# Normalization, gate chain and convolution sums rewritten in the front of a two-layer hybrid block

## Chip, cores and metric

The kernel runs on one core of a Trainium2 chip. The metric is the device time of one execution in microseconds (us); where several executions were timed, their median counts.

## The reference, cut to what matters

512 tokens (256 context, 256 latent) of width 1024 go through two layers. In the second layer the context is only read, so everything after the keys and values is computed for the 256 latent tokens alone. Each layer is

```python
h = rmsnorm(x, norm1_g) * (1.0 + sc1) + sh1
a, mq, mk, mv, mo, mg, dq, dk, dv = jnp.split(h @ w_in, splits, axis=-1)
conv_l = conv_module(a, conv_w, conv_b, conv_ln_g, conv_ln_b)
mlstm_l = mlstm_mixer(...)            # gates: ig + bias, log_sigmoid(fg + bias), scans over time
diff_l = diff_mixer(...)
x = x + g1 * (jnp.concatenate([conv_l, mlstm_l, diff_l], axis=-1) @ w_out)
h2 = rmsnorm(x, norm2_g) * (1.0 + sc2) + sh2
x = x + g2 * peer_ffn(h2, peer_wq, peer_keys, peer_u, peer_v)
```

The convolution module is a depthwise convolution of 31 taps over time on 256 channels, followed by a layer norm and SiLU:

```python
u = a[..., :CONV_W] * jax.nn.sigmoid(a[..., CONV_W:])
y = lax.conv_general_dilated(u, conv_w, ...) + conv_b      # 31 taps, one filter per channel
return jax.nn.silu(layernorm(y, ln_g, ln_b))
```

The modulation vectors sc1, sh1, g1, ... are products of a conditioning vector with six 1024 x 1024 blocks of a matrix ("ada").

## The kernel before

Activations lie with channels on the 128 partitions and tokens along the free axis: `x[:, c, t]` is chunk c (of 8) of 128 channels, and a "half" is 256 tokens, so one operation of the norm has the shape 128x256. Every product runs in split precision: an operand v is kept as hi = v rounded to fp32r and lo = v - hi, and TensorE makes three matmuls of 128x512 or 128x256 (hi x hi, lo x hi, hi x lo) for each chunk. `wsplit` (L210) makes the two parts of a weight block: ScalarE writes whi (L218), GpSimd subtracts to give wlo (L219), one pair for each 128x512 half block. A Tile scheduler orders the instructions of each engine when the program is built, and each engine then works through its own list in that order.

Each layer has a front (`front`, L346) and an expert stage (`peer`). The front does, in order:

- `norm_mod` (L276 to L286): for each of 8 chunks and each half, four operations on four engines' turns: VectorE multiplies x by the reciprocal root (L282), ScalarE applies scale and shift (L283), GpSimd copies the result, rounded, to hh (L284), VectorE subtracts to give hl (L285). It is called twice per layer: n1 ahead of the input projection, n2 ahead of the expert stage (two halves for n1 of both layers and n2 of layer 0, one half for n2 of layer 1).
- `projg`: the four first blocks of the projection (gates, two blocks of convolution gates, one of convolution values) together, into banks "f", "f", "f", "d" of PSUM; matmuls L311 to L313.
- `gate_rows` (L488 to L553): the gates' block (128x512 in PSUM, of which 64 rows are input gates and 64 forget gates) becomes log-sigmoid sums. VectorE adds the bias (L497) and moves the forget rows down (L498), ScalarE takes Abs, Exp, Ln, Exp (L500 to L506), VectorE forms the log sigmoid (L502 to L509), splits it and the input gate into hi and lo by adding and subtracting a constant (L513 to L515), runs scans (L524, L528) and subtracts (L532, L533). TensorE then transposes the two results (L548); a second path makes `rows` (L542), which the mLSTM reads through the matmul at L590. Its scratch T1 shares the buffer of "v", T2 that of "vx".
- Further projections (`proj`, L297 to L299), among them the output gates and, in layer 0 only, `late()` (L1159), which computes three blocks of the modulation with `ada_rows` (L181) through the PSUM bank "a".
- `conv` (L460 to L485): for each of two blocks b of 128 channels one tensor_scalar (L465) and 30 scalar_tensor_tensor (L468) on VectorE, each adding one shifted and weighted copy of `up` to the sum cy in SBUF (128x512 in layer 0, 128x256 in layer 1); then TensorE sums over channels (L472), and the layer norm follows.
- `mlstm`: per head rows,sel (L590), the exponentials E (L598 ScalarE, L602 VectorE, L604, GpSimd's mask L606), the products mq,km (L611), VectorE's E times product (L616), the sums E,vx (L622). Then `diff`, `w_out` with the residual (L443) and sums of squares, and `norm_mod` again.

The order of these steps is the string 'kmcvkk0k123' (k keys, m mLSTM, c convolution, v values, digits the heads of differential attention), and the scheduler interleaves them. PSUM in the front has eight banks: f three, d two, m two, a one. The lines that the change touches are L282 to L285, L460 to L475, L488 to L517 and L1161.

## Time and profile before

| | us |
|---|---|
| median of 3 runs | 2994.78 (2994.21 to 3012.2) |
| the profiled execution, its own time | 3002.47 |
| span of the profiled execution, first to last instruction | 3000.3 |
| TensorE busy in the span | 2884.3 (96%) |
| mean granted TensorE clock | 0.981 |

The fronts of the two layers lie at about 0 to 430 us and 1915 to 2215 us of the span, the expert stages behind each. In the rows, PE is TensorE's matmuls, PEld its weight loads, DVE VectorE, ACT ScalarE, POOL GpSimd. "hh, whi" are operands by the program's names; f, d, m and a are the four kinds of PSUM bank. A matmul's duration overlaps with its neighbours', so the distance of two starts is what one costs.

### The profile page before, as it was taken

What the parts mean: (1) busy time and instruction counts of PE and PEld (TensorE: products, weight loads), DVE (VectorE), ACT (ScalarE), POOL (GpSimd) and SP (SyncE); (2) the same over time, 40 slices, a digit from 0 to 9 for tenths busy, and PEclk for the clock granted to TensorE, in tenths of its full rate; (3) what the DMA queues carried; (4) which work ended last, traced back from release to release, by engine and by line L of the source; (5) the groups of instructions that cost most, each with busy time, mean ns of one, the idle gap of its engine ahead of it and who ended that gap; (6) DMA issues with size and microseconds to landing.
All of it is one profiled execution on the core that took longest, in us unless ns stands there. A gap on an engine that the chain in (4) does not pass through costs nothing.

```text
span 3000.3 us, 43088 instructions
## 1 busy us (share of the span) xinstructions
PE 2884.3 (96%) x14960; PEld 2409.7 (80%) x14960; DVE 2009.4 (67%) x4447; ACT 1422.2 (47%) x2862; POOL 1075.4 (36%) x887
## 2 busy tenths in 40 slices
PE   7899999999999999999999999989989999999998
PEld 4575578888888888888888888777789999888887
DVE  4956537875666665566666665586659888666665
ACT  4344443336566665332333323345455666555554
POOL 4333255566666666000000000253478877000000
PEclk9899899999999999999999999999999999999999
DMA  6511134444555555867677776121255877998873
GB/s 234 189 64 36 35 113 137 127 137 164 211 183 204 189 188 213 283 238 249 235 242 239 242 247 216 34 83 52 78 178 175 277 255 272 309 314 270 267 233 125
DMA packets 257866, 565.60 MB, mean 189 GB/s; under 512 B 18336, under 2 KB 119200, under 8 KB 254448
## 3 DMA queue, kind: packets, MB, share of 16 engines
q1 hardware_dynamic: 256928, 560.42, 55.3%
q8 instruction: 118, 1.93, 0.3%
q0 software_dynamic: 720, 2.43, 0.2%
q14 instruction: 100, 0.82, 0.1%
HBM read 464.21 MB, written 98.57 MB: 188 GB/s over the span
## 4 chain that ended last, share of the span: by engine, by line
PE 76%; DVE 7%; DMA 1%; POOL 1%; ACT 1%; issue 1%; SPq 0%; DVEq 0%; ACTq 0%; POOLq 0%
PE h L864 10%; PE h L865 10%; PE h L866 10%; PE acc L1138 8%; PE acc L1139 8%; PE acc L1140 8%; PE acc L969 4%; PE acc L970 4%; PE acc L971 4%; PE f L813 3%; DVE cy L468 1%; PE f L311 1%; PE f L312 1%; PE f L313 1%; DMA v<-in_peer_v 1%
## 5 line engine op out<-in xcount | busy, mean ns | idle before, releaser
L847 POOL TENSOR_TENSOR ul<-u,uh 128x512 fp32r<-128x512 f32 x464 | 610.5, 1325 | 335.0 <-ACT uh L846 317.1
L864 PE MATMUL h<-hh,uh 128*128 128x512 f32 (+1 forms) x2048 | 692.4, 338 | 2.6 <-ACT ga L870 2.5
L866 PE MATMUL h<-hh,ul 128*128 128x512 f32 (+1 forms) x2048 | 689.6, 337 | 5.2 <-POOL ul L847 5.2
L865 PE MATMUL h<-hl,uh 128*128 128x512 f32 (+1 forms) x2048 | 689.9, 337 | 0.0
L846 ACT ACTIVATE uh<-u 128x512 fp32r<-128x512 f32 x512 | 319.3, 629 | 468.6 <-PE h L865 345.7
L866 PEld LDWEIGHTS h<-hh,ul 128*128 128x128 f32 x2048 | 389.5, 190 | 46.6 <-POOL ul L847 5.7
L864 PEld LDWEIGHTS h<-hh,uh 128*128 128x128 f32 x2048 | 389.9, 190 | 43.6 <-ACT ga L870 4.2
L865 PEld LDWEIGHTS h<-hl,uh 128*128 128x128 f32 x2048 | 389.9, 190 | 37.0
L1138 PE MATMUL acc<-vh,wh 128*128 128x512 f32 x1024 | 398.6, 389 | 1.1 <-ACT ga L870 1.1
L1139 PE MATMUL acc<-vl,wh 128*128 128x512 f32 x1024 | 398.6, 389 | 0.0
L1140 PE MATMUL acc<-vh,wl 128*128 128x512 f32 x1024 | 398.5, 389 | 0.0
L815 DVE TENSOR_REDUCE rt_stg<-f 128x256 f32<-128x512 f32 x384 | 244.9, 686 | 225.2 <-PE f L813 224.4
L219 POOL TENSOR_TENSOR wlo<-wt,whi 128x512 fp32r<-128x512 f32 x164 | 231.1, 1420 | 247.2 <-ACT whi L218 231.0
L1103 ACT ACTIVATE wh<-gb 128x512 fp32r<-128x512 f32 x128 | 80.7, 632 | 463.3 <-PE acc L1139 451.4
L375 POOL MEMSET up<- 128x60 f32 (+1 forms) x2 | 0.3, 148 | 718.0 <-PE acc L991 718.0
L1104 DVE TENSOR_TENSOR wl<-gb,wh 128x512 fp32r<-128x512 f32 x128 | 88.8, 695 | 236.9 <-ACT wh L1103 236.8
L1138 PEld LDWEIGHTS acc<-vh,wh 128*128 128x128 f32 x1024 | 192.2, 188 | 41.4 <-ACT ga L870 1.5
L1140 PEld LDWEIGHTS acc<-vh,wl 128*128 128x128 f32 x1024 | 192.2, 188 | 39.8
L1139 PEld LDWEIGHTS acc<-vl,wh 128*128 128x128 f32 x1024 | 192.2, 188 | 39.7
L846 ACT ACTIVATE vh<-v 128x512 fp32r<-128x512 f32 x256 | 155.7, 626 | 140.8 <-PE acc L971 81.4
L801 DVE SCALAR_TENSOR_TENSOR rt_oh_g<-iotap,rt_sT,rt_sg 128x256 fp32r<-128x256 f32 x512 | 213.3, 474 | 0.1
L969 PE MATMUL acc<-vh,wh 128*128 128x512 f32 x512 | 198.9, 390 | 1.3 <-ACT vh L846 1.3
(322 smaller groups left out, 5417.8 us busy)
## 6 DMA issues: line engine op xcount, KB each, us to landing
u<-in_peer_u SPq DMA_DIRECT2D x256, 512.0 KB, 4.0
v<-in_peer_v SPq DMA_DIRECT2D x256, 512.0 KB, 5.0
G<-rt_stg SPq DMA_DIRECT2D x24, 2048.0 KB, 6.9
act<-ga SPq DMA_DIRECT2D x180, 256.0 KB, 2.9
gb<-act SPq DMA_DIRECT2D x180, 256.0 KB, 3.7
g<-G SPq DMA_DIRECT2D x32, 1024.0 KB, 5.5
wa<-in_ada_t SPq DMA_DIRECT2D x56, 512.0 KB, 4.4
w<-in_ada_w SPq DMA_DIRECT2D x20, 1024.0 KB, 6.0
```

The source lines that it names most:

```text
L219: nc.gpsimd.tensor_sub(lo, raw, hi)
L801: nc.vector.scalar_tensor_tensor(og[:, k], self.iotap[:, None, :].to_broadcast([128, 2, 128]), sT[:, 1, c:c + 1], sg[:, c, :, None].bitcas ...
L815: nc.vector.tensor_reduce(stg[:, :, t4 + k2:t4 + k2 + 2].rearrange("p j t -> p t j"), pg.rearrange("p (t x j) -> p t j x", t=2, x=2), axis ...
L846: nc.scalar.activation(hi, raw[:, k * 512:(k + 1) * 512], AF.Copy)
L847: lo_eng.tensor_sub(lo, raw[:, k * 512:(k + 1) * 512], hi)
L864: nc.tensor.matmul(o, uh, hh[:, c, c0:], start=c == 0, stop=False)
L865: nc.tensor.matmul(o, uh, hl[:, c, c0:], start=False, stop=False)
L866: nc.tensor.matmul(o, ul, hh[:, c, c0:], start=False, stop=c == NB - 1)
L969: nc.tensor.matmul(A, wh[:, t], vh, start=s0, stop=False)
L1138: nc.tensor.matmul(A, wh[:, t], vh, start=s0, stop=False)
L1139: nc.tensor.matmul(A, wh[:, t], vl, start=False, stop=False)
L1140: nc.tensor.matmul(A, wl[:, t], vh, start=False, stop=s1)
```

## The change

The norm is made in three operations: VectorE forms x times A times the reciprocal root (one scalar_tensor_tensor), ScalarE adds the shift B and writes hh rounded, VectorE forms (u + B) - hh. GpSimd has no part in it.

The convolution adds up its taps in PSUM bank "a" instead of cy. In layer 0 each block b needs a whole bank, so the second block's sums begin when ScalarE has copied the first block's to cy; in layer 1 both blocks share one bank. ScalarE copies each sum to cy (Copy, two per layer).

The gate chain reads the PSUM block directly: ScalarE's Abs with the bias, VectorE twice at 64 rows (input gate + bias; forget gate + bias, minimum with 0). The input gate is split ahead of the log sigmoid; three later operations are merged into others. The scratch lies in two tiles of the buffer "PT" instead of that of "vx".

The late modulation of layer 0 uses the PSUM banks "d" instead of "a".

```diff
--- before.py
+++ after.py
@@ -279,10 +279,9 @@
         for c in range(NB):
             for o, t, s in self.halves(c0):
                 u = self.w(T, "nm", fam="r")
-                nc.vector.tensor_mul(u, self.x[:, c, t], rs[o])
-                nc.scalar.activation(u, u, AF.Identity, bias=B[:, c, s:s + 1], scale=A[:, s, c:c + 1])
-                nc.gpsimd.tensor_scalar(hh[:, c, t], u, 1.0, 0.0, op0=OP.mult, op1=OP.add)
-                nc.vector.tensor_sub(hl[:, c, t], u, hh[:, c, t])
+                nc.vector.scalar_tensor_tensor(u, self.x[:, c, t], A[:, s, c:c + 1], rs[o], op0=OP.mult, op1=OP.mult)
+                nc.scalar.activation(hh[:, c, t], u, AF.Identity, bias=B[:, c, s:s + 1])
+                nc.vector.scalar_tensor_tensor(hl[:, c, t], u, B[:, c, s:s + 1], hh[:, c, t], op0=OP.add, op1=OP.subtract)
         return hh, hl
 
 
@@ -461,12 +460,16 @@
         nc = self.nc
         ys = [self.frontp.tile([128, n], F32, name=f"cy{b}") for b in range(2)]
         for b in range(2):
-            y = ys[b].rearrange("p (s t) -> p s t", t=T)
+            if n * b % 512 == 0:
+                bank = self.ps("a")
+            sums = bank[:, n * b % 512:n * b % 512 + n]
+            y = sums.rearrange("p (s t) -> p s t", t=T)
             nc.vector.tensor_scalar(y, up[:, b, :, 0:T], P["conv_w"][:, b, 0:1], P["conv_b"][:, b:b + 1],
                               op0=OP.mult, op1=OP.add)
             for k in range(1, CONV_K):
                 nc.vector.scalar_tensor_tensor(y, up[:, b, :, k:k + T], P["conv_w"][:, b, k:k + 1], y,
                                          op0=OP.mult, op1=OP.add)
+            nc.scalar.activation(ys[b], sums, AF.Copy)
         mu = self.ps("a")[:, :n]
         for b in range(2):
             nc.tensor.matmul(mu, self.ones, ys[b], start=b == 0, stop=b == 1)
@@ -490,31 +493,31 @@
 
         nc, F = self.nc, self.frontp
         T1 = F.tile([128, 4, TT], F32, name="gr1", tag="v")
-        T2 = F.tile([64, 4, TT], F32, name="gr2", tag="vx")
-        G = T1[:, 0]
+        T2, T3 = (F.tile([64, 2, TT], F32, name=k, tag="PT", bufs=2) for k in ("gr2", "gr3"))
         Fg, e, u = (T1[0:64, k] for k in (1, 2, 3))
-        r, L, Bl, M = (T2[:, k] for k in range(4))
-        nc.vector.tensor_scalar(G, ps, P["gate_b"][:, 0:1], None, op0=OP.add)
-        nc.vector.tensor_copy(Fg, G[64:128])
-        ig = G[0:64]
-        nc.scalar.activation(e, Fg, AF.Abs)
+        r, L, Bl, M = T2[:, 0], T2[:, 1], T3[:, 0], T3[:, 1]
+        b = P["gate_b"]
+        nc.scalar.activation(e, ps[64:128], AF.Abs, bias=b[64:128, 0:1])
         nc.scalar.activation(e, e, AF.Exp, scale=-1.0)
-        nc.vector.tensor_scalar(u, e, 1.0, None, op0=OP.add)
-        nc.scalar.activation(L, u, AF.Ln)
-        nc.vector.tensor_scalar(r, u, -1.0, None, op0=OP.add)
-        nc.vector.tensor_sub(r, e, r)
-        nc.scalar.activation(u, L, AF.Exp, scale=-1.0)
-        nc.vector.tensor_mul(r, r, u)
-        nc.vector.tensor_add(L, L, r)
-        nc.vector.scalar_tensor_tensor(L, Fg, 0.0, L, op0=OP.min, op1=OP.subtract)
-        lh, ll, ih, il = e, u, r, Fg
+        ig = T1[0:64, 0]
+        nc.vector.tensor_scalar(ig, ps[0:64], b[0:64, 0:1], None, op0=OP.add)
+        nc.vector.tensor_scalar(Fg, ps[64:128], b[64:128, 0:1], 0.0, op0=OP.add, op1=OP.min)
 
         def split(hi, lo, v):
             nc.vector.tensor_scalar(hi, v, SPLIT, None, op0=OP.add)
             nc.vector.tensor_scalar(hi, hi, SPLIT, None, op0=OP.subtract)
             nc.vector.tensor_sub(lo, v, hi)
+        ih, il = r, ig
+        split(ih, il, ig)
+        nc.vector.tensor_scalar(u, e, 1.0, None, op0=OP.add)
+        nc.scalar.activation(L, u, AF.Ln)
+        nc.vector.scalar_tensor_tensor(e, u, -1.0, e, op0=OP.add, op1=OP.subtract)
+        nc.scalar.activation(u, L, AF.Exp, scale=-1.0)
+        nc.vector.tensor_mul(e, e, u)
+        nc.vector.tensor_sub(L, L, e)
+        nc.vector.tensor_sub(L, Fg, L)
+        lh, ll = e, u
         split(lh, ll, L)
-        split(ih, il, ig)
 
         def scan(dst, src, op):
             for d in range(2):
@@ -1158,7 +1161,7 @@
 
                 def late():
                     for w in (2, 4, 3):
-                        self.ada_rows(0, P[0], w, ("kT", "qT"), "a", "a")
+                        self.ada_rows(0, P[0], w, ("kT", "qT"), "d", "d")
                 h = self.front(l, P[l], c0, late if l == 0 else None)
 
             def side():
```

In the rows below and in the prediction the line numbers are those of the kernel before; in lists of the changed kernel they are one lower between the norm and the convolution's head (L296 for L297) and three higher behind it (L593 for L590). gr is the gates' scratch, ident the identity for the transposes, up the padded convolution input, a the PSUM bank.

VectorE, layer 1, from the gates' first operation to the middle of the chain. Before:

```order
L497 TENSOR_SCALAR gr_17497<-f,small_127 128x512
L498 COPY gr_17497<-gr_17497 64x512
L382 TENSOR_TENSOR up<-d,sg 128x256
L465 TENSOR_SCALAR cy_18305<-up,small_127 128x256
L468 SCALAR_TENSOR_TENSOR cy_18305<-up,small_127,cy_18305 128x256 x4
L502 TENSOR_SCALAR gr_17497<-gr_17497 64x512
L382 TENSOR_TENSOR up<-f,sg 128x256
L504 TENSOR_SCALAR gr_17498<-gr_17497 64x512
L468 SCALAR_TENSOR_TENSOR cy_18305<-up,small_127,cy_18305 128x256
L505 TENSOR_TENSOR gr_17498<-gr_17497,gr_17498 64x512
```

The same place of the changed kernel:

```order
L503 TENSOR_SCALAR gr_17453<-f,small_127 64x512
L504 TENSOR_SCALAR gr_17453<-f,small_127 64x512
L507 TENSOR_SCALAR gr_17454<-gr_17453 64x512
L512 TENSOR_SCALAR gr_17453<-gr_17453 64x512
L508 TENSOR_SCALAR gr_17454<-gr_17454 64x512
L514 SCALAR_TENSOR_TENSOR gr_17453<-gr_17453 64x512
L509 TENSOR_TENSOR gr_17453<-gr_17453,gr_17454 64x512
L381 TENSOR_TENSOR up<-d,sg 128x256
L467 TENSOR_SCALAR a<-up,small_127 128x256
L381 TENSOR_TENSOR up<-f,sg 128x256
```

The split of the input gate (L507 to L509) now stands at the front of the chain, ahead of the first tap, and only 8 taps instead of 11 stand between the chain's first operation and the subtraction that the transposes wait for (L532, now L535).

TensorE, layer 1, about the start of the mLSTM (rows,sel). Before:

```order
L590 MATMUL m<-rows,sel 128x256 x2
L472 MATMUL a<-cy_18305,ones 128x256
L472 MATMUL a<-cy_18306,ones 128x256
L339 MATMUL f<-rp_t,perm 128x256
L297 MATMUL f<-hh,whi 128x256
```

The changed kernel, the same place, and the rows to which the convolution's sums over channels went:

```order
L593 MATMUL m<-rows,sel 128x256 x2
L338 MATMUL f<-rp_t,perm 128x256
L296 MATMUL f<-hh,whi 128x256
...
L625 MATMUL m<-E,vx 128x256
L593 MATMUL m<-rows,sel 128x256
L328 MATMUL f<-wlo,hh 128x256
L475 MATMUL a<-cy_18261,ones 128x256
L475 MATMUL a<-cy_18262,ones 128x256
```

The two matmuls that read cy moved 51 rows back, behind the first head's sums E,vx.

TensorE, layer 1, about the first transposes of the gates. Before:

```order
L297 MATMUL f<-hh,whi 128x512
L298 MATMUL f<-hl,whi 128x512
L548 MATMUL m<-ident,gr_17498 128x64 x4
L299 MATMUL f<-hh,wlo 128x512
L297 MATMUL f<-hh,whi 128x512
```

After the change, the row of the transposes and its neighbours:

```order
L297 MATMUL f<-hl,whi 128x512
L298 MATMUL f<-hh,wlo 128x512
L551 MATMUL m<-ident,gr_17454 128x64 x4
L296 MATMUL f<-hh,whi 128x512
L297 MATMUL f<-hl,whi 128x512
```

The transposes stand 8 projection matmuls earlier in layer 1 (behind 18 of the 128x512 matmuls that lie behind the 128x256 ones instead of 26) and 9 earlier in layer 0.

VectorE, layer 1, the taps behind `rows` in the changed kernel; before, 43 taps of both blocks stood here in turn, and then the layer norm's first operation (L474) ahead of the first E (L602):

```order
L545 TENSOR_TENSOR rows<-gr_17453,rows 64x1024
L470 SCALAR_TENSOR_TENSOR a<-up,small_127,a 128x256 x17
L467 TENSOR_SCALAR a<-up,small_127 128x256
L470 SCALAR_TENSOR_TENSOR a<-up,small_127,a 128x256 x24
L340 TENSOR_TENSOR rp_u<-f,rope 128x256
L605 TENSOR_SCALAR E<-m,ah 128x128
```

The last six taps of the second block stand behind the first E, between operations of the mLSTM.

## Rows read from the trace of the kernel before

**Rows 1.** Page, busy time, share of the span and instructions of each engine.

```profile
PE 2884.3 (96%) x14960; PEld 2409.7 (80%) x14960; DVE 2009.4 (67%) x4447; ACT 1422.2 (47%) x2862; POOL 1075.4 (36%) x887
```

**Rows 2.** Windows: stretch, its length, busy us of each engine, PEclk, DMA share, GB/s.

```profile
0.00:430.00 430.00, 375.41 (x1639) 257.17 (x1640) 262.11 (x480) 191.78 (x414) 164.32 (x184) 0.93 0.33 115
430.00:1900.00 1470.00, 1467.67 (x6772) 1221.99 (x6771) 956.67 (x2257) 633.79 (x1297) 479.27 (x337) 1.00 0.60 203
1900.00:2230.00 330.00, 287.38 (x1692) 242.40 (x1692) 217.35 (x453) 162.88 (x339) 163.68 (x159) 0.94 0.26 81
...
150.00:175.00 25.00, 24.93 (x121) 18.88 (x121) 6.69 (x15) 9.82 (x24) 12.13 (x11) 1.00 0.27 85
...
2020.00:2040.00 20.00, 13.21 (x63) 10.23 (x63) 15.61 (x27) 8.35 (x22) 11.57 (x13) 0.83 0.36 105
```

**Rows 3.** Waits of PE, 0 to 430: us in total, times, longest.

```profile
PE m L548 <- DVE gr L532: 8.8, 1, 8.8
PE f L311 <- POOL hh L284: 8.7, 2, 6.0
```

**Rows 4.** Waits of PE, 1900 to 2230, the same columns.

```profile
PE m L548 <- DVE gr L532: 11.3, 1, 11.3
PE f L311 <- POOL hh L284: 9.4, 2, 5.2
PE a L472 <- DVE cy L468: 6.8, 1, 6.8
PE f L311 <- ACT rt_q L690: 3.1, 2, 2.9
```

**Rows 5.** Timeline 1935.8 to 1945: start, us, engine, instruction, idle before and releaser.

```profile
1935.91 1.97 DVE L282 TENSOR_TENSOR nm<-x,rsx 128x256 f32<-128x256 f32 x5
1936.38 2.57 ACT L283 ACTIVATE nm<-nm,mod,A 128x256 f32<-128x256 f32 x5 [2.64 <-DVE nm L282]
1937.06 2.69 POOL L284 TENSOR_SCALAR hh<-nm 128x256 fp32r<-128x256 f32 x5 [1.98 <-ACT nm L283]
...
1938.20 0.80 PE L311 MATMUL f<-hh,whi 128*128 128x512 f32 x1 [5.21 <-POOL hh L284]
...
1941.30 0.63 PE L311 MATMUL f<-hh,whi 128*128 128x512 f32 x1
1941.73 0.63 PE L312 MATMUL f<-hl,whi 128*128 128x512 f32 x1
...
1944.60 0.39 PE L311 MATMUL f<-hh,whi 128*128 128x512 f32 x1
1944.82 0.39 PE L312 MATMUL f<-hl,whi 128*128 128x512 f32 x1
```

**Rows 6.** Timeline of DVE, 1960 to 2031, the same columns.

```profile
1961.14 0.75 DVE L497 TENSOR_SCALAR gr<-f,small 128x512 f32<-128x512 f32 x1 [7.93 <-PE f L313]
...
1964.16 2.05 DVE L468 SCALAR_TENSOR_TENSOR cy<-up,small,cy 128x256 f32<-128x256 f32 x4
...
1978.30 2.88 DVE L514 TENSOR_SCALAR gr<-gr 64x512 f32<-64x512 f32 x2
1981.10 2.35 DVE L515 TENSOR_TENSOR gr<-gr,gr 64x512 f32<-64x512 f32 x2
...
1988.30 0.68 DVE L532 TENSOR_TENSOR gr<-gr 64x512 f32<-64x512 f32 x1
...
2001.78 27.95 DVE L468 SCALAR_TENSOR_TENSOR cy<-up,small,cy 128x256 f32<-128x256 f32 x43
```

**Rows 7.** Timeline of POOL, 1955 to 2032, the same columns.

```profile
2013.99 8.59 POOL L219 TENSOR_TENSOR wlo<-wt,whi 128x512 fp32r<-128x512 f32 x3 [5.58 <-ACT whi L218]
```

**Rows 8.** Lines, 1900 to 2230: xcount, busy us, mean ns, idle before.

```profile
L468 DVE SCALAR_TENSOR_TENSOR cy<-up,small,cy 128x256 f32<-128x256 f32 x60 | 39.5, 702 | 0.6
L616 DVE SCALAR_TENSOR_TENSOR E<-m,ea,E 128x256 f32<-128x256 f32 x24 | 10.6, 478 | 5.2 <-PE m L611 4.6 <-POOL E L606 0.7
...
L237 DVE TENSOR_SCALAR m<-m 128x256 f32<-128x256 f32 x7 | 3.0, 430 | 8.3 <-ACT y L236 8.3
```

## The prediction

> **What bounds the kernel now.** I read the page's busy times first, then the windows, then TensorE's waits stretch by stretch, then timelines of the places that the waits name. TensorE is busy 96% of the span [rows 1]. The windows show where the missing 4% is: between 430 and 1900 us it is busy 1467.67 of 1470.00 us at a granted clock of 1.00 and nothing that other engines do can be worth anything there; in the two fronts it is busy 375.41 of 430.00 and 287.38 of 330.00 at clocks of 0.93 and 0.94 [rows 2]. So the change, all of which lies in the fronts (and in the norm ahead of each expert stage), can only win from some 97 us of idle time (54.6 and 42.6) and from the lower clock.
>
> TensorE's waits in the fronts say which of that the change can reach: 8.8 and 11.3 us for the gates' subtraction ahead of the transposes, 8.7 and 9.4 for GpSimd's hh of the norms (two waits each), 6.8 for the convolution sums in layer 1, 3.1 for the routing's rt_q [rows 3, 4]. These are 48.1 us. The rest of the idle time (loads, squares, the differential attention) is not touched.
>
> A long wait has a second price. [...] Some twelve matmuls are run so, at about 0.2 us extra each: 2.4 us. After the convolution's wait the clock of the 20 us is 0.83 [rows 2].
>
> **The change part by part.**
>
> *Norm.* In the chain at 1935.91 VectorE gives over to ScalarE after 0.47 us, ScalarE to GpSimd after 0.68, GpSimd to TensorE after 1.14 [rows 5]. The step through GpSimd goes, and ScalarE must now hand over to TensorE, which costs it something between its 0.68 and GpSimd's 1.14. So 0.68 to 1.14 us goes from each of four starts; with 0.7 in layer 1 and 1.1 in layer 0, where GpSimd also has a wlo in its list ahead of hh, I count 0.7, 0.8, 1.1, 1.1. The rest of the 8.7 and 9.4 us is the reciprocal root ahead of it, which stays. VectorE's two operations get a pointer operand; the tap, which has one too, takes 0.51 us for the shape [rows 6], so I set this at nothing. Behind the last norm ScalarE's shorter list should bring rt_q earlier: between 0 and 3.1 us [rows 4], I take 1.5.
>
> *Gates.* From the first operation at 1961.14 to the end of the subtraction, 1988.98, VectorE has 27.8 us of work and hardly an idle moment [rows 6]. In the lists 33 instructions stand in this stretch before and 29 after: one gate operation less (0.68 us, the price of L532) and three taps less (at the mean 0.70, [rows 8], 2.1). The other eight taps go from 0.70 to the undisturbed 0.51 if PSUM frees them from what slows them now (next part): 1.5. Sum 4.3. The splits still take and give SBUF and can stay as slow as the 2.88 and 2.35 us for two [rows 6]; if they speed up as well, to 0.68 each at most, another 2.5. The ScalarE waits of the chain are filled by the input gate's split. So the subtraction is early by 2.8 (taps as slow as now) to 6.8 us, I take 4.3, plus the norm's 0.7: 5.0. But TensorE now does 8 matmuls less ahead of the transposes, and does them after, at 0.22 to 0.43 us [rows 5]: 1.8 to 3.4 back. Net for layer 1, norm included: 2.4 us. Layer 0, with a norm that gives 1.1 and 9 matmuls (2.0 to 3.9) moved: also 2.4. The wait in the profile will so look hardly shorter, about 9 us.
>
> *Convolution, layer 1.* TensorE comes to the sums over channels at about 2022.9 and waits to 2029.7 for a run of 43 taps that began at 2001.78 and took 27.95 us, 0.65 each [rows 4, 6]. Undisturbed, four take 2.05, 0.51 each [rows 6]. In the changed list 42 operations of it stand behind `rows`, starting 5.0 us earlier, at 1996.8; at 0.51 they end at 2018.2. TensorE, 2.4 us earlier, comes at 2020.5, and no longer for them but for the first E, which is behind them on VectorE. Slack 2.3 us. The wait of 6.8 goes, and with it the slow clock behind it, about 2.5 (as worked out above). What comes back: six taps (3 us) between operations of the mLSTM, the two matmuls and the layer norm later in it; VectorE is not full there, so I take 2 of loss. Net 7.3.
>
> What a tap in a PSUM bank costs no row shows. An operation that reads and writes PSUM in place takes 430 ns at 128x256, one with one PSUM and one SBUF tensor and a pointer 478 [rows 8], against 510 for the tap in SBUF. From below it is 0.43, from above what a tap takes now with GpSimd busy, 0.70. I take 0.51, the nearer in kind.
>
> Why are the taps slow now? The mean of all 60 is 702 ns [rows 8] against 510, and where they overlap GpSimd's wlo, GpSimd is slowed too: three took 8.59 us [rows 7]. The two engines hold each other up. [...]
>
> [...]
>
> *Convolution, layer 0.* TensorE does not wait for these sums now. Their second half is held until ScalarE has copied the first out of the bank, and 62 taps stand ahead of the first E. Between 150 and 175 us VectorE is busy 6.69 of 25 us [rows 2], so there is cover of up to 18 us, of which part lies behind the E's; I reckon with 3 us of it and a cost of nothing, at worst 5.
>
> *Late modulation* moves from bank "a" to "d", which differential attention needs only later: nothing, at worst a wait of one operation, 0.7 us (the price of L532, [rows 6]).
>
> **Sum.** Layer 0: 2.4 and 1.1 for the second norm. Layer 1: 2.4, 7.3, 0.8 for the second norm, 1.5 for rt_q. Together 15.5 us off the profiled execution's 3002.47: 2987.0. That execution lies 7.7 above the median of 2994.78, so the median becomes 2979.
>
> **Rivals.**
> - *The taps stay slow.* If PSUM does not free them, 42 at 0.70 end at 2026.2, TensorE waits 5.7 us at the first E and the slow clock (2.5) comes back: 15.5 less 8.2 is 7.3, time 2987 (2994.8 less 7.3). For it: the splits in the same stretch, which stay in SBUF, suffer as much [rows 6]. Against it: the operation on E that reads PSUM has a mean of 478 [rows 8], although GpSimd is busy half of that stretch [rows 2].
> - *The waits only move.* The chain of the gates has as many dependent steps as before, and its transposes merely stand earlier; if the layer norm and the first E's then come late as well, some 2 us remain: 3000.5 for this execution, 2993. For it: the same list of scans stands ahead of the transposes. Here the change doesn't do what it says.
> - *The waits go altogether*, if the delays by GpSimd vanish everywhere and TensorE is never slowed: 48.1 us and three slow stretches of 2.4: 55 us, 2940. Against it: the reciprocal root ahead of hh and the scans (L524, L528) stay.
> - *Slower: a tap onto PSUM is dear,* since each reads what the one before has just written to the same bank. A surcharge of d costs 42 d less 2.3 in layer 1 and 62 d less 3 in layer 0; it uses up the 15.5 us at d = 0.20 us (a tap of 0.71). At d = 0.4 the kernel is 21 us longer: 3016. Against it: the in-place row of 430 ns [rows 8]; that row is of single operations, not of a chain.
>
> **Numbers.** Forecast 0.45; taps stay slow 0.25; waits move 0.13; all waits go 0.09; dear taps 0.08. A measurement of this kernel can tell about 1%, 30 us, from no change (its three runs span 18). Faster by more than that needs the third rival, or it in part: 0.10. Slower by more needs d above 0.5: 0.04. The rest, 0.86, lies within 1%. The range takes in the first two rivals and most of the way to the third: 2960 to 3000.
>
> **What would show it.** Right: no wait of TensorE for a cy in layer 1; taps of 128x256 at 0.5 us also while wlo runs; transposes at about 1984 with a wait of about 9 us; hh by ScalarE about 0.7 us earlier; in 2020 to 2040 a clock near 1.00. Wrong: taps of 0.7 or more; a new wait of TensorE for E at the start of the mLSTM; gate operations that wait for ScalarE; norms whose last operation on VectorE becomes what TensorE waits for.

## The result, and the profile after

The changed kernel takes 2987.48 us in the median of 13 runs (2979.22 to 2997.42), the kernel before, timed beside it, 3008.67 us (13 runs, 2994.21 to 3014.57). The ratio is 0.994 with a 95% interval of 0.9925 to 0.9955: 0.6% faster. On the median that the prediction started from (2994.78) that is 2977; forecast were 2979 and a range of 2960 to 3000. The profiled execution takes 2984.03 us, 18.4 less than the one of before; the working had given 15.5. So the sum holds. How it came about holds only in part, and that the total agrees so well is partly luck: as the table below shows, the terms of layer 0 and of the last norm were too small and those of layer 1 too large.

The executions of each program spread over some 20 us, with the mean granted clock of TensorE that a run lists (0.977 to 0.985 for the kernel before in the comparisons below, 0.979 to 0.986 for the changed kernel); so most comparisons below are made inside a profile, and between runs of like clock.

TensorE's waits of the changed kernel, 0 to 430 us (us in total, times, longest); they answer to [rows 3]:

```profile
PE f L249 <- ACT sq L248: 13.1, 3, 6.6
PE f L310 <- ACT hh L283: 6.2, 2, 5.0
PE m L551 <- DVE gr L535: 5.8, 1, 5.8
```

The same from 1880 to 2230 us, against [rows 4]:

```profile
PE m L551 <- DVE gr L535: 8.6, 1, 8.6
PE f L310 <- ACT hh L283: 8.1, 2, 4.6
PE m L673 <- DVE df_p L670: 5.9, 4, 2.7
```

The wait for cy is gone, hh now comes from ScalarE, the gates' two waits are 3.0 and 2.7 us shorter, and rt_q is no longer in the list. In third place df_p now stands (the softmax weights of differential attention), with 5.9 us where it had 2.4.

The norm's chain in layer 1, timeline (start, us, engine, instruction), against [rows 5]:

```profile
1927.36 1.28 DVE L282 SCALAR_TENSOR_TENSOR nm<-x,A,rsx 128x256 f32<-128x256 f32 x3
1927.88 1.31 ACT L283 ACTIVATE hh<-nm,mod 128x256 fp32r<-128x256 f32 x3 [2.90 <-DVE nm L282]
...
1928.84 1.22 PE L310 MATMUL f<-hh,whi 128*128 128x512 f32 x2 [4.61 <-ACT hh L283]
```

From VectorE's start to TensorE's it is 1.48 us, before 2.29. ScalarE hands over to TensorE after 0.96 us, between the 0.68 and 1.14 that the prediction bounded it by.

VectorE in the gates and the taps of layer 1, timeline, against [rows 6]:

```profile
1952.01 0.74 DVE L503 TENSOR_SCALAR gr<-f,small 64x512 f32<-64x512 f32 x1 [6.27 <-ACT gr L500]
...
1961.78 1.38 DVE L518 TENSOR_TENSOR gr<-gr,gr 64x512 f32<-64x512 f32 x1
1963.09 0.47 DVE L470 SCALAR_TENSOR_TENSOR a<-up,small,a 128x256 f32<-128x256 f32 x1
...
1970.19 2.10 DVE L527 TENSOR_TENSOR_SCAN gr<-gr,zero 32x512 f32<-32x512 f32 x1
...
1974.51 0.68 DVE L535 TENSOR_TENSOR gr<-gr 64x512 f32<-64x512 f32 x1
...
1986.76 8.94 DVE L470 SCALAR_TENSOR_TENSOR a<-up,small,a 128x256 f32<-128x256 f32 x17
...
1996.73 12.56 DVE L470 SCALAR_TENSOR_TENSOR a<-up,small,a 128x256 f32<-128x256 f32 x24
```

Between its neighbours in SBUF, which GpSimd still draws out (L518 1.38 us, undisturbed 0.68; the scan at 1970.19 2.10 us, undisturbed 1.21), a tap takes 0.47. The taps behind `rows` end at 2009.3, TensorE comes to rows,sel at 2008.76. The stretch from the first gate operation to the subtraction takes 23.2 us, before 27.8.

Lines of the changed kernel, 1880 to 2230 us (xcount, busy us, mean ns, idle before), against [rows 8]:

```profile
L470 DVE SCALAR_TENSOR_TENSOR a<-up,small,a 128x256 f32<-128x256 f32 x60 | 29.2, 487 | 1.7
...
L284 DVE SCALAR_TENSOR_TENSOR hl<-nm,mod,hh 128x256 fp32r<-128x256 f32 x24 | 13.1, 596 | 2.5 <-ACT hh L283 2.5
...
L282 DVE SCALAR_TENSOR_TENSOR nm<-x,A,rsx 128x256 f32<-128x256 f32 x16 | 9.9, 668 | 0.0
```

A tap costs 487 ns (before 702). The norm's first operation, still with two tensors in SBUF, takes 668 (before 489), its last 596 (before 748): together about as much as before.

Where the 18 us are, from the starts of the same instructions in both timelines:

| from, to | before | changed | difference |
|---|---|---|---|
| start, first hh matmul of layer 0 | 40.5 | 40.0 | -0.5 |
| to the last norm's first matmul, layer 0 | 357.2 | 347.1 | -10.1 |
| expert stage of layer 0, to the first norm of layer 1 | 1540.5 | 1541.8 | 1.3 |
| first norm of layer 1 to its last norm | 247.0 | 243.6 | -3.4 |
| to the end | 815.1 | 809.8 | -5.3 |

The prediction had put 3.5 into layer 0, 10.5 into the front of layer 1 and 1.5 behind its last norm. Layer 0 gave three times its share, the front of layer 1 a third. Inside layer 1 the mLSTM's first mq,km does start 9.7 us earlier after its norm (2035.06 - 1938.20 against 2015.95 - 1928.84), where the working had 11.0 (1.7 from the gates, 9.3 from the sums) before it took off 2 of loss; 6.3 of it is gone by the last norm.

### The profile page after: what moved, and what is told of

Its sections match the earlier page's. It is cut to its first block, busy times and chain, and to the rows that moved or that the text cites. A ratio compares the mean times of both kernels' runs of the same rounds, so it can differ in the third digit from the quotient of the medians.

```text
span 2982.2 us, 43006 instructions
## 1 busy us (share of the span) xinstructions
PE 2881.3 (97%) x14960; PEld 2408.4 (81%) x14960; DVE 1990.6 (67%) x4445; ACT 1411.4 (47%) x2861; POOL 1040.4 (35%) x831
## 4 chain that ended last, share of the span: by engine, by line
PE 77%; DVE 6%; DMA 1%; POOL 1%; ACT 1%; issue 1%; SPq 0%; DVEq 0%; ACTq 0%; POOLq 0%
PE h L867 10%; PE h L868 10%; PE h L869 10%; PE acc L1141 8%; PE acc L1142 8%; PE acc L1143 8%; PE acc L973 4%; PE acc L972 4%; PE acc L974 4%; PE f L816 3%; PE f L310 1%; PE f L311 1%; PE f L312 1%; DMA u<-in_peer_u 1%; POOL ul L850 1%
## 5 line engine op out<-in xcount | busy, mean ns | idle before, releaser
L869 PEld LDWEIGHTS h<-hh,ul 128*128 128x128 f32 x2048 | 389.6, 190 | 46.7 <-POOL ul L850 5.7
L868 PEld LDWEIGHTS h<-hl,uh 128*128 128x128 f32 x2048 | 390.0, 190 | 36.9
L1141 PE MATMUL acc<-vh,wh 128*128 128x512 f32 x1024 | 399.3, 390 | 1.8 <-ACT ga L873 1.8
L219 POOL TENSOR_TENSOR wlo<-wt,whi 128x512 fp32r<-128x512 f32 x164 | 227.4, 1399 | 266.9 <-ACT whi L218 260.3
L850 DVE TENSOR_TENSOR vl<-v,vh 128x512 fp32r<-128x512 f32 x256 | 170.1, 687 | 44.1 <-ACT vh L849 43.5
```

The source lines that it names most:

```text
L219: nc.gpsimd.tensor_sub(lo, raw, hi)
L850: lo_eng.tensor_sub(lo, raw[:, k * 512:(k + 1) * 512], hi)
L868: nc.tensor.matmul(o, uh, hl[:, c, c0:], start=False, stop=False)
L869: nc.tensor.matmul(o, ul, hh[:, c, c0:], start=False, stop=c == NB - 1)
L1141: nc.tensor.matmul(A, wh[:, t], vh, start=s0, stop=False)
```

## The experiments

Twelve runs, two of them without an edit. The first four take the parts apart: only the norm, only the gate chain, only the sums in PSUM with the late modulation, and all but these sums.

### Only the norm

```diff
-                nc.vector.tensor_mul(u, self.x[:, c, t], rs[o])
...
+                nc.vector.scalar_tensor_tensor(u, self.x[:, c, t], A[:, s, c:c + 1], rs[o], op0=OP.mult, op1=OP.mult)
+                nc.scalar.activation(hh[:, c, t], u, AF.Identity, bias=B[:, c, s:s + 1])
...
```

> Kernel before with only the new norm (three operations). If the parts are worth what the prediction gave them: hh about 0.7 to 1.1 us earlier at each of the four norm starts, rt_q's wait shorter, together 3.7 to 5.2 us (0.12 to 0.17% faster); the waits for the gates (8.8 and 11.3 us) and for cy in layer 1 (6.8 us) stay within 1 us. Rival, that the norm's list on VectorE and GpSimd is what made layer 0 gain 10.6 us instead of 3.5: 8 us or more, with the start of layer 0's last norm at 390 us or earlier instead of 397.7.

Ratio to before 0.997 (0.995 to 0.9989); median 3001.19. That is 9 us, more than the 3.7 to 5.2 expected, but its interval reaches from 3 to 15. TensorE still waits for the sums:

```profile
PE a L471 <- DVE cy L467: 6.7, 1, 6.7
```

The last norm of layer 0 starts at 396.0, so the norm alone is not what shortened layer 0.

### Only the gate chain

```diff
-        T2 = F.tile([64, 4, TT], F32, name="gr2", tag="vx")
...
+        T2, T3 = (F.tile([64, 2, TT], F32, name=k, tag="PT", bufs=2) for k in ("gr2", "gr3"))
...
+        nc.scalar.activation(e, ps[64:128], AF.Abs, bias=b[64:128, 0:1])
...
+        split(ih, il, ig)
...
```

> Kernel before with only the new gate chain and its scratch. If the shorter chain by itself gives the gates' gain: transposes near 1980 in layer 1 (before 1989.0) and near 89 in layer 0 (before 94.7), 6 to 10 us in all. Rival, that the gates were late because of slow taps between their operations: transposes only 2 to 3 us earlier in each layer, under 4 us in all. The wait for cy in layer 1 stays (5 us or more), since the taps in SBUF stay at about 0.70 us.

Ratio 0.9975 (0.9952 to 0.9998). Its waits from 1890 to 2230 us:

```profile
PE a L472 <- DVE cy L468: 5.7, 1, 5.7
...
PE f L311 <- ACT rt_q L690: 3.0, 1, 3.0
```

The transposes come 4.2 us earlier behind the first norm in layer 0 and 2.1 in layer 1 (table below). Layer 0 meets the first expectation (transposes at 88.88), layer 1 the second; the 6.3 us together are at the low end of the first. Its profile shows something that I had not looked for: the last norm of layer 0 starts at 380.58, 17 us earlier than before, though the transposes come only 5.8 earlier. In layer 0 the new chain also changed TensorE's list: the first mq,km stands 122 matmuls earlier in it than before, in the changed kernel 130.

### Only the sums in PSUM

```diff
+            if n * b % 512 == 0:
+                bank = self.ps("a")
...
+            nc.scalar.activation(ys[b], sums, AF.Copy)
...
-                        self.ada_rows(0, P[0], w, ("kT", "qT"), "a", "a")
+                        self.ada_rows(0, P[0], w, ("kT", "qT"), "d", "d")
```

> Kernel before with only the sums in PSUM (and the late modulation in the banks d). Forecast: taps 0.49 us at 128x256, no wait for cy, 7 to 8 us from layer 1's mLSTM start, nothing in layer 0. Rival, that the taps delay the gates: besides this the transposes 2 to 4 us earlier in each layer, 10 to 14 us in all. If the sums only move the wait: under 3 us.

Ratio 0.995 (0.9925 to 0.9974), the largest of the parts. No wait for cy is left; what leads the list from 1890 to 2230 us is

```profile
PE f L311 <- ACT rt_q L694: 3.4, 1, 3.4
```

From the transposes to the first mq,km it takes 36.9 us in place of 46.0. The transposes themselves come 1.4 and 1.7 us earlier: the rival has a small part of it. Of the 10.8 us that mq,km is early behind its norm, 3.5 are left at the last norm of layer 1 (table below). The profiled execution as a whole is only 0.6 us shorter than that of before (spans 2999.7 and 3000.3, clocks 0.980 and 0.981).

### Norm and gates, sums as before

```diff
-            if n * b % 512 == 0:
-                bank = self.ps("a")
...
+            y = ys[b].rearrange("p (s t) -> p s t", t=T)
```

> Changed kernel with the convolution and the late modulation as before (norm and gates new). If the parts add up: the whole of 18 us less what the sums alone gave, 8 to 12 us faster than before, with the wait for cy back in layer 1. If the parts only work together (one list of VectorE): under 5 us.

Ratio 0.9954 (0.9933 to 0.9975), which is 14 us where 8 to 12 were expected, and the wait is back:

```profile
PE a L471 <- DVE cy L467: 5.7, 1, 5.7
```

By the ratios the parts do not seem to add up: 0.3, 0.25 and 0.5% alone, 0.46% for norm and gates, 0.6% for all; the sum of the three, 1.05%, is above 0.6 by little more than the intervals allow. Runs of like mean clock say the same (mean us, number of runs; the runs of before from three comparisons together):

| mean clock of the run | before | norm | gates | sums | norm and gates | all |
|---|---|---|---|---|---|---|
| 0.984 to 0.986 | 2994.2 (4) | 2989.9 (2) | 2989.2 (5) | 2981.4 (4) | 2982.0 (2) | 2982.8 (5) |
| 0.979 to 0.981 | 3010.4 (18) | 3002.6 (10) | 3005.8 (5) | 3001.5 (5) | 3000.0 (3) | 2994.6 (4) |

Norm 4 to 8 us, gates 5, sums 9 to 13, but all together 11 to 16. What the sums add to norm and gates is not told apart from nothing by the intervals. And runs of the same program lie 12 to 20 us apart between the two lines.

The stretches inside the profiles are steadier, since they do not hold the whole run's clock (us between starts):

| kernel | norm to transposes, layer 0 | the same, layer 1 | transposes to first mq,km, layer 1 | first to last norm, layer 0 | the same, layer 1 |
|---|---|---|---|---|---|
| before, twice | 54.2, 54.3 | 50.8, 49.7 | 46.0, 47.0 | 357.2, 361.8 | 247.0, 246.7 |
| norm | 52.7 | 50.5 | 46.0 | 358.1 | 247.4 |
| gates | 50.0 | 48.7 | 47.6 | 341.7 | 248.1 |
| sums | 52.8 | 49.2 | 36.9 | 355.8 | 243.5 |
| norm and gates | 48.5 | 47.7 | 47.7 | 339.7 | 246.4 |
| changed, twice | 46.7, 46.8 | 46.4, 46.4 | 40.7, 38.8 | 347.1, 347.0 | 243.6, 241.8 |

The last two columns say where the parts end up: layer 0 is shortened above all with the gates, layer 1 with the sums and not with the gates. In the profiles of the gates alone and of norm and gates layer 0 also lacks a slow stretch of the clock, worth some 12 us, that the others have (next section).

### The clock in layer 0: the same programs again

The profile of the gates alone differs from before in one stretch above all. Windows of before (stretch, length, busy us of PE, PEld, DVE, ACT, POOL, PEclk, DMA share, GB/s):

```profile
280.00:310.00 30.00, 28.24 (x78) 14.67 (x77) 19.76 (x41) 11.02 (x32) 8.47 (x10) 0.75 0.07 18
```

of the changed kernel:

```profile
280.00:310.00 30.00, 28.70 (x60) 13.38 (x59) 14.74 (x36) 9.37 (x26) 3.17 (x4) 0.60 0.00 1
```

and of the gates alone:

```profile
280.00:310.00 30.00, 28.01 (x99) 13.94 (x99) 24.10 (x54) 16.64 (x46) 6.41 (x7) 1.00 0.07 18
```

TensorE is busy in all three, with 78, 60 and 99 matmuls. In the first two the granted clock is at half for some 24 us (290 to 320 us before, 280 to 310 in the changed kernel, 0.50 in the middle 10 us of each), with no wait over 1.3 us ahead; in the third it is 1.00. The slow stretch begins right behind a wait of 1.3 us for df_p (matmul starts at 294.9 and 285.2 us); the gates alone have the same wait (1.29 us, at 288.7) without it. This is differential attention, and none of the change is in it. The profile of norm and gates is at 1.00 there as well. Two runs without an edit ask whether the program or the execution decides.

> The kernel before, a second profile. In the six profiles so far TensorE's clock in the differential attention of layer 0 (about 280 to 325 us) is at 0.50 to 0.84 for some 30 us in before, norm only, sums only and changed, and near 1.00 in gates only and gates with norm. If that depends on the program, this profile shows the fall again between 290 and 320 and layer 0's last norm starts at 396 to 399 us. If it depends on the execution, it may be missing: last norm at about 384 to 388, span about 2988.

> The changed kernel, a second profile. If the low clock at 280 to 310 us depends on the program: there again, last norm of layer 0 at 386 to 388 us. If on the execution: it may be missing, last norm at about 374 to 377, span about 2970. The waits for the gates' subtraction (5.8 and 8.6 us) come again within 0.5 us, and so does the one of 2.7 us for df_p in layer 1, if it comes from the order of the list.

Both fell again: the clock was 0.60 and 0.50 in 300 to 320 us of before, 0.69, 0.50 and 0.62 in 280 to 310 of the changed kernel, with the last norm of layer 0 at 402.1 and 385.33, both just outside what was expected (the first has a second slow stretch, 0.64 in 240 to 250 us). So in these two programs it comes again. But gates alone ran from 2987 to 3010 us with clocks from 0.979 to 0.986, which its one profile (0.986) does not stand for: there the execution has a say too. What decides is left open. The waits of 5.8, 8.7 and 2.7 us came again as expected. The two spans of this pair, 3007.1 and 2975.9 us, differ by 31 where the first pair differed by 18: one pair of profiles does not give the change's worth to 10 us.

### Why the taps were slow: GpSimd without its reads

```diff
-            nc.gpsimd.tensor_sub(lo, raw, hi)
+            nc.gpsimd.memset(lo.bitcast(F32), 0.0)
```

> Kernel before in which GpSimd fills wlo with zeros instead of subtracting: the low parts of the front's weights are left out, and GpSimd writes SBUF but no longer reads it there. If the taps in SBUF are slow because GpSimd reads SBUF beside them: 0.48 to 0.52 us at 128x256 on the mean (before 0.702), about 0.73 at 128x512 (before 0.855), the pairs L514 and L515 at 0.75 and 1.25, no wait or under 1 us for cy in layer 1. If a tap in SBUF is slow by itself: 0.65 us or more.

2929.27 us (one run), mean clock 0.992, with the source of the kernel before otherwise; the scheduler also orders some of TensorE's matmuls anew. Lines, 0 to 2230 us:

```profile
L219 POOL MEMSET wlo<- 128x512 f32 x164 | 87.0, 534 | 288.1 <-PE f L299 140.7 <-PE d L313 75.4 <-PE f L330 31.0
...
L468 DVE SCALAR_TENSOR_TENSOR cy<-up,small,cy 128x512 f32<-128x512 f32 x60 | 42.3, 745 | 0.5
L468 DVE SCALAR_TENSOR_TENSOR cy<-up,small,cy 128x256 f32<-128x256 f32 x60 | 25.8, 477 | 0.6
```

The taps in SBUF take 477 and 745 ns here, as fast as those in PSUM (487 for the smaller). GpSimd still writes in every one of these 164 operations, for a shorter time (534 ns in place of 1395 in layer 0 and 1436 in layer 1 of the kernel before). Instruction by instruction the cause shows more sharply than in the means. In layer 1 of the kernel before, 28 of the 60 taps lie for more than half of their time beside a wlo subtraction and take 962 ns on the mean, the 28 that lie beside none 474. In this run 13 lie so beside a write of zeros and take 481 ns; in the changed kernel 32 lie so beside a full subtraction and take 487. So the mean of 702 was a mixture of undisturbed taps and held-up ones, and beside an operation that only writes nothing was lost. No wait for cy is left, and the span (2927.6) is 73 us shorter than that of before: far more than the taps.

### Both kinds of tap in one program

```diff
-            sums = bank[:, n * b % 512:n * b % 512 + n]
+            sums = ys[b] if b else self.ps("a")[:, :n]
```

> Changed kernel in which only the convolution's first block adds up in PSUM, the second in SBUF. If GpSimd's reads slow taps with two SBUF inputs alone: first block 0.48 to 0.50 us at 128x256, second 0.6 to 0.8 on the mean, in the same run and the same stretch. If PSUM makes no difference: both alike within 0.05.

Lines, 0 to 2230 us, first the SBUF block, then the PSUM block:

```profile
L468 DVE SCALAR_TENSOR_TENSOR cy<-up,small,cy 128x512 f32<-128x512 f32 x30 | 26.5, 882 | 0.3
L468 DVE SCALAR_TENSOR_TENSOR cy<-up,small,cy 128x256 f32<-128x256 f32 x30 | 23.7, 789 | 0.4
...
L468 DVE SCALAR_TENSOR_TENSOR a<-up,small,a 128x512 f32<-128x512 f32 x30 | 22.3, 744 | 0.1
L468 DVE SCALAR_TENSOR_TENSOR a<-up,small,a 128x256 f32<-128x256 f32 x30 | 14.3, 475 | 0.0
```

Beside GpSimd's full subtraction a tap with one tensor in SBUF is not delayed (475 ns), one with two is, by 0.31 us at 128x256 (789). The wait for cy is back with 6.2 us. The one run takes 2995.47 us at a clock of 0.979, about as much as the changed kernel's runs of such a clock (2994.6), and from the first norm of layer 1 to its last it takes 242.4 us, the changed kernel 243.6 and 241.8: here the wait costs nothing that is left at the last norm.

### What is left, and a version that beats both

If VectorE loses that much to GpSimd's wlo, VectorE may as well make wlo itself: 164 operations on two SBUF tensors, with no subtraction of GpSimd's beside them.

```diff
-            nc.gpsimd.tensor_sub(lo, raw, hi)
+            nc.vector.tensor_sub(lo, raw, hi)
```

> Changed kernel with the whole subtraction for wlo on VectorE instead of GpSimd. If what the fronts still lose is VectorE held up by GpSimd's reads: its operations on two SBUF tensors go to their undisturbed times (0.68 us at 64x512), the waits for the gates fall from 5.8 and 8.6 us to about 3 and 4 as with the zeros, and the kernel is 10 to 30 us faster than the changed one (0.3 to 1.0%). Rival, that VectorE becomes the bound in the fronts (some 113 us of work more on an engine busy 254 of 430 and 225 of 330): TensorE waits for wlo, 5 to 30 us slower.

Median 2939.26 us (2938.11 to 2939.59), ratio to before 0.977 (0.9741 to 0.9799): 2.3% faster than before and, by the two ratios to before, 1.7% faster than the change. Lines, 0 to 2190 us, and waits, 1850 to 2190 us:

```profile
L219 DVE TENSOR_TENSOR wlo<-wt,whi 128x512 fp32r<-128x512 f32 x164 | 114.1, 711 | 70.6 <-ACT whi L218 60.1 <-PE f L311 6.0 <-PE d L311 3.1
```

```profile
PE f L310 <- ACT hh L283: 7.4, 2, 3.7
PE m L551 <- DVE gr L535: 2.6, 1, 2.6
...
PE f L298 <- DVE wlo L219: 0.7, 1, 0.7
```

VectorE makes a wlo in 0.711 us where GpSimd took 1.4; the wait for the gates is 2.6 us in place of 8.6, and TensorE waits 0.7 for wlo. The four runs lie within 1.5 us of each other, all at a mean clock of 0.991: the fall of the clock in layer 0 is not there (1.00 from 250 to 340 us in its windows). The 48 us between this median and that of the changed kernel (2987.48, from another comparison) are above the 10 to 30 expected; some 20 of them go with the mean clock (an estimate: 0.984 to 0.991 of 2940 us), which was not counted.

With every second half block on VectorE:

```diff
-            nc.gpsimd.tensor_sub(lo, raw, hi)
+            (nc.vector if k else nc.gpsimd).tensor_sub(lo, raw, hi)
```

> Changed kernel with every second half block's wlo on VectorE. First theory: about half the gain of the version with all of them, 5 to 15 us faster than the changed kernel. Rival: the two engines still hold each other up, within 4 us of the changed kernel.

2952.64 us, ratio 0.9818 (0.9788 to 0.9848): more than half of it and above the 5 to 15 us expected, and the gates' wait in layer 1 still 6.0. VectorE's 82 wlo have a mean of 875 ns here, with GpSimd's 82 beside them.

### The change without GpSimd's reads

The same zeros for wlo in the changed kernel, and in the kernel before, timed together:

> Changed kernel in which GpSimd fills wlo with zeros instead of subtracting (the low parts of the weights are left out). If the sums in PSUM win only because they escape GpSimd's reads, the change is worth little here: 0 to 6 us beside the kernel before with the same zeros, from the norms and the shorter chain. If PSUM or the shorter lists win by themselves: 10 us or more.

> Kernel before with the same zeros for wlo, timed beside the one above: median near 2930, clock about 0.99. It is the base for the difference that the run above is to give.

2924.73 us (2924.19 to 2926.55) against 2933.88 (2931.37 to 2934.12): 9.2 us, between the two expectations. In both profiles no wait for cy is listed; the norms' waits are 13.0 against 16.3 us, the gates' 6.3 against 6.5. So nothing of the sums' gain is left in the waits. By the starts in the two profiles the difference lies in layer 0 (314.6 against 322.2 us from the first norm to the last), where the granted clock is 0.994 and 0.966; the front of layer 1 is 1.8 us longer than its base's (221.0 against 219.2). The cause of the clock I have not separated.

These two runs also bear on the 6.3 us that the changed kernel loses behind mq,km. In this front the changed kernel with zeros has TensorE's 1194 matmuls in the same order as without. From mq,km to the last norm it takes 141.5 us with 1.7 us of waits, its base 140.4 with 1.9; with GpSimd's subtractions the changed kernel takes 156.5 with 14.5, the kernel before 150.1 with 9.7. VectorE's last operation on df_p there (lines, 1880 to 2230 us), in the changed kernel and then in the one with zeros:

```profile
L670 DVE SCALAR_TENSOR_TENSOR df_p<-df_p,df_z,df_p 128x512 f32<-128x512 f32 x8 | 10.2, 1272 | 0.1
L670 DVE SCALAR_TENSOR_TENSOR df_p<-df_p,df_z,df_p 128x512 f32<-128x512 f32 x8 | 6.0, 748 | 0.1
```

## Why the prediction was right, and where its steps were not

*The sum* (15.5 us, a time of 2979) was right within what can be measured: 0.6%. The forecast case, the likeliest, is the one that came, and of the rivals the dear taps are ruled out (487 ns), and so is the one that the taps stay slow. That the waits only move holds in part: it is what layer 1 does with two thirds of its gain. But the agreement of the total is partly luck. Against 3.5, 10.5 and 1.5 us stand 10.6 in layer 0 (with the start), 3.4 in the front of layer 1 and 5.3 behind it, and 1.3 lost in the expert stage between: two errors of some 7 us cancel.

*Norm:* forecast 0.7 and 0.8 in layer 1 and 1.1 twice in layer 0. Measured: 0.6 for layer 1's first norm (behind the end of the expert stage) and 0.5 for layer 0's (from the start), and for the last ones, behind the last sums of squares, 1.0 in layer 0 (9.6 to 8.6 us) and 0.7 in layer 1 (5.3 to 4.6). Together 2.8 of 3.7: the mechanism is right, and the term of layer 0's first norm was twice too large. That the operations with a pointer cost nothing holds for the two together (668 and 596 ns, before 489 and 748), not for L282 alone, which still reads two tensors in SBUF beside GpSimd; with wlo made by VectorE it takes 479.

*rt_q:* 1.5 taken of a range to 3.1. The wait is gone, and the stretch from the last norm to the end is 5.3 us shorter, with 809.8 us in both profiles of the changed kernel; 4.3 of it lie ahead of the first matmul into h (L864, 32.1 and then 27.8 us behind the norm). The wait stays in the gates alone and in the sums alone (3.0 and 3.4 us) and is gone in the norm alone. There, though, only 2.0 us are won up to that matmul (30.1), with a wait of 1.8 for wlo in its place, and in this profile the whole stretch to the end is 824.9 us, longer than before. So the norm alone removes the wait, but it does not give the 5.3. This term was mis-sized by some 3 us. The sum had left out the clock here: in the first pair of profiles it was at half for 7.9 us behind the last norm before, 3.4 of them right behind the wait for rt_q, and for 3.4 in the changed kernel; in the second pair it was 6.0 and 5.2, with no fall behind the wait.

*Gates:* in layer 1 the transposes were to come 4.3 us earlier behind the norm; they come 4.4 earlier. But to the last norm of layer 1 nothing of this is left in the gates alone (248.1 us, before 247.0) and 0.5 in norm and gates, where 2.4 were forecast. In layer 0 the transposes come 7.4 earlier, with 17 matmuls less ahead of them (9 of the projection, which were counted, and 8 of the late modulation, which were not). The whole way to the last norm is 10.1 us shorter, so the term of 2.4 us was too small there. The runs give the parts up to the transposes: norm 1.5, gates 4.2, sums 1.4. Behind them a wait of 2.6 us for the first E (L602) is gone, which the working had not priced; TensorE's idle time from 0 to the last norm falls from 53.9 to 46.5 us, and the granted clock over it rises from 0.927 to 0.935, some 4 us (an estimate from the two). As forecast the wait shrinks less than the chain (to 8.6 us, 9 was said).

*Convolution:* 0.51 forecast for a tap in a run of several, 0.52 measured (24 in 12.56 us; a single tap takes 0.487), and no wait for cy. The slack of 2.3 us was not there: the taps behind `rows` end 0.5 us after TensorE's rows,sel, but no wait for the first E followed. The mechanism of the taps is shown twice: taps in SBUF become as fast when GpSimd does not read (477), and in one program the block in PSUM is free of the delay and the block in SBUF is not (475 and 789). That a tap in PSUM would be free of GpSimd was my assumption, for which the rows had only the 478 ns of the operation on E; these runs show it for the taps (32 of them beside a subtraction take 487 ns). It does not follow for every operation with one tensor in SBUF: L514, a tensor_scalar that reads one there, takes 1.48 us in layer 1 before, beside GpSimd, and 0.41 undisturbed. Nor is the tap dearer for its source in PSUM: 475 to 487 ns there against 477 undisturbed in SBUF. The slow clock behind a wait, some twelve matmuls at 0.2 us extra, is seen behind the norm's wait of 5.21 us in the kernel before (twelve take 5.66 us from 1938.20 on, 2.74 from 1944.60 on). Behind the wait for cy it was taken at 2.5 us: there the matmuls start at half their later rate for 2.9 us in the first profile of before (from 2029.78 on) and for 5.3 in the second (from 2034.04 on), some 1.4 and 2.6 us lost (estimates from these stretches). Without that wait the clock is 1.00 from 2000 to 2050 us in the sums alone and in the second profile of the changed kernel, but 0.83 in 2010 to 2020 of its first, some 1.7 us: one pair of profiles shows the term, the other does not.

*The step that failed* is "What comes back: ... I take 2 of loss". Of the 9.7 us that the mLSTM starts earlier, 6.3 are lost again before layer 1's last norm, in the second pair of profiles 6.6 of 11.5, in the sums alone 7.3 of 10.8. So the term of 7.3 us for the convolution came to 2.9 and 4.6 beside norm and gates (by the two profiles of the changed kernel) and to 3.5 alone. One place shows a part of it. Timeline of the changed kernel:

```profile
2081.05 1.12 PE L660 MATMUL d<-kT,qT 64*128 64x512 f32 x2
2084.86 0.47 PE L673 MATMUL m<-ident,df_p 128*128 128x128 f32 x1 [2.69 <-DVE df_p L670]
```

In the fixed order of its list TensorE meets this transposition of df_p ahead of 24 projection matmuls that do not depend on it, with VectorE a softmax behind; it waits 2.69 us, and the clock is 0.83 in 2080 to 2090. Before, 24 such matmuls stood between the score matmuls (2098.60) and the transposes (2105.69). The waits for df_p rise from 2.4 to 5.9 us. All waits between mq,km and the last norm rise by 4.8 us (9.7 to 14.5), in the second pair by 1.9 (10.8 to 12.7). But df_p is not the whole of it: in the sums alone its waits are 2.3 us, and as much is lost. Nor is the order of the list enough: with zeros for wlo the same list takes 1.0 us longer here than its base's. So the loss stood only where GpSimd's subtractions ran beside VectorE; which of the operations held up makes it stays open.

*Not in the sum at all* was the clock away from the edits. The slow stretch in layer 0's differential attention costs about 12 us (an estimate from three windows of 10 us at 0.76, 0.50 and 0.54 before, at 0.77, 0.50 and 0.54 in the changed kernel). Both profiles have it, so it takes no part in their difference of 18; but it is as large as the change, the gates alone, norm and gates, and the versions in which GpSimd subtracts less or not at all do not show it, and by it a time can go either way.

## What to carry to other kernels

When an engine's operations on SBUF have two prices in a trace, ask which other engine runs in the dear ones. Moving their sums to PSUM cured 120 taps (855 to 752 ns at 128x512, 702 to 487 at 128x256); moving the other engine's 164 subtractions, which drew out other operations too, gave 1.7% where the sums alone gave 0.5. And what a gain at one wait is worth shows only at the next place that all the work must pass, here the last norm: compare the starts there, over two profiles, before believing it.

## What the runs showed of the hardware that I had not expected

- The fronts' GpSimd subtraction costs far more than the waits that carry its name (TensorE's are 2.9 us in the changed kernel). Made by VectorE (711 ns for a 128x512, GpSimd 1399), it leaves a median 48 us lower, with VectorE at 285 of the first 400 us busy.
- A mean of 702 ns can stand for no operation at all: a tap of 128x256 in layer 1 took 474 ns beside no subtraction of GpSimd's and 962 on the mean (up to 1604) beside one.
- TensorE's clock fell to half (0.50 in 300 to 310 us before) in a stretch where it hardly waits (longest wait 1.3 us, busy 28.24 of 30 us); in the gates alone, with another order of TensorE's list ahead of it and the same wait, it stayed at 1.00 in the one profile.
- Scans can be drawn out by GpSimd as other operations on two SBUF tensors are: 2.10 us for the one at 1970.19, 1.21 undisturbed (L518: 1.38, undisturbed 0.68).
